# One 512-column product for a weight block's high half and both halves of the activations

## The chip, the core and the metric

The kernel runs on one core of a Trainium2 chip. The metric is the time of one execution on the device in microseconds (us). Inside the core five engines work side by side, each through its own queue in order: PE (TensorE, matrix products; PEld is its weight loads), DVE (VectorE), ACT (ScalarE), POOL (GpSimd) and SP (here the queue that issues the DMAs).

## The reference

Two layers over 256 tokens of width 2048. Each layer has a mixer sub-layer (two attentions, gates, projections) and a feed-forward with a depthwise convolution of width 3; both take an input that is RMS-normalised and modulated by the conditioning vector `c` (adaLN). The change lies in the feed-forward alone:

```python
h = rmsnorm(x, norm_ffn[l]) * (1.0 + sc_m) + sh_m
u = depthwise_conv(h @ w_up[l], conv_w[l], conv_b[l])   # 2048 -> 2 x 5632
g, v = jnp.split(u, 2, axis=-1)
x = x + gt_m * ((jax.nn.silu(g) * v) @ w_down[l])       # 5632 -> 2048
```

All inputs are float32.

## The kernel before

**Layout.** Activations lie with features on the 128 partitions and the 256 tokens (`S`) along the row, in chunks of 128 features. Weights come as blocks of 128 x 128; 16 blocks (1 MB) are a *unit*, loaded by one DMA into a tile `w` (line 335) of a pool of four, which the adaLN weights share. A layer's units follow each other in the order in which the products use them (`block_stream`); a layer has 232 units, and its feed-forward is units 100 to 231.

**Two halves.** To keep float32 accuracy from the faster fp32r products, each operand is split in a high half (rounded) and a low half (the rest). For weights `unit_steps` does this in two pieces of 8 blocks: ACT casts the high half (line 346), DVE subtracts to get the low half (line 347), both into a tile `hl`, of which there are four, so two units' worth. A block's contribution is high x high + high x low + low x high: three products of 256 columns in `feature_block` (lines 375 to 377), accumulated over the blocks of one output column in one of four PSUM tiles `ps`. The activation operand is read "turned": columns alternate between the first and the second 128 tokens (`turns`), and the sums come back by `turned_back` or are already in order (`sorted`).

**The feed-forward.** The 44 chunks of hidden features go in three groups of 14, 17 and 13. A group's up-projection takes for each chunk a g column and a v column of 128 features, 16 blocks each, so one unit a column. Evacuation of a column (`g_evac`, `v_evac`, `conv`): ACT computes u = w1 ps + b (line 1096), DVE adds the two neighbour taps by two multiply-adds (line 1098); for g, ACT applies silu (1126); for v, DVE multiplies by silu(g) (1131), and `split` makes the two halves of `act` (ACT 452, DVE 455). The group's down-projection then runs over the 16 output chunks, the first three together, and DVE adds each to the residual stream `x` (`residual`, line 1071). The first 12 of the 28 columns of the first group work on `bare`, the input before normalisation, with two extra columns for the shift (258, 256 and 258 columns); the rest use the normalised `h`. The feed-forward's last group in layer 0 also feeds the squares and the bare chunks for the next layer; in layer 1 each output chunk is stored by a DMA.

**The order.** A scheduler in the framework sorts the instructions when the program is built; each engine's queue then runs in that order. The adaLN weights `aw` of layer 1 stream in by a plan of counts by unit (`ADA_PLAN_0`: 80 by unit 108, 143 by unit 231), each followed by a DVE product of 128 x 2048 (line 246).

Of the kernel before, what the change touches and what calls it, by code (L numbers as in the profile page):

```python
# [9 lines left out]
F32 = mybir.dt.float32  # L10
F32R = mybir.dt.float32r
AF = mybir.ActivationFunctionType
ALU = mybir.AluOpType
AX = mybir.AxisListType

P = 128
L = 2
D = 2048
S = 256
# [65 lines left out]

SCORES_3 = (1,)
EARLY = {1: 2}

MOVED_QK = [(), (0,1,2,8)]
QK_STEPS = 3  # L90
# [53 lines left out]
def encoder(ctx: ExitStack, tc: tile.TileContext, a: dict, out: bass.AP):  # L144
    nc = tc.nc
# [13 lines left out]
    ev = pool("ev", 3)  # L159
# [30 lines left out]
    sp = pool("s", 1)  # L190
# [13 lines left out]
    def led(name, apart=None):  # L204

        t = hp.tile([P, KC * 2 * S + OFF + ROW], F32R, name=name, tag="h")
        at = [0] + [OFF + 2 * S * k for k in range(1, KC)]
        if apart:
            at[apart] += ROW - OFF
            at[apart + 1 :] = [i + ROW for i in at[apart + 1 :]]  # L210
        return [t[:, i : i + 2 * S].rearrange("p (a s) -> p a s", a=2) for i in at]
# [55 lines left out]
    class Paced:  # L267


        def __init__(self):  # L270
            self.jobs, self.later = [], []
# [87 lines left out]
    def turns(columns):  # L359

        return columns.rearrange("p (r q) -> p q r", r=2)

    def turned_back(columns):

        return columns.rearrange("p (q r) -> p r q", r=2)

    def pair(columns):

        return columns.rearrange("p (r q) -> p r q", r=2)

    def feature_block(ps, hl, j, act, first, last):

        hi, lo = hl[:, 0, j * P : (j + 1) * P], hl[:, 1, j * P : (j + 1) * P]
        out = ps[:, : 2 * act[0].shape[1]]
        nc.tensor.matmul(out, hi, act[0], start=first, stop=False)  # L375
        nc.tensor.matmul(ps[:, :S], hi, act[1], start=False, stop=False)  # L376
        nc.tensor.matmul(out, lo, act[0], start=False, stop=last)  # L377

    class Stream:
# [33 lines left out]
        def features(self, acts, evacs, late=None, at={}, sorted=False):  # L413

            pss = [mm.tile([P, 512], F32, name=f"ps{self.l}_{self.u}_{self.at}_{m}", tag="mm") for m in range(len(evacs))]
            for i, act in enumerate(acts):
                if late and i == len(acts) - LATE:
                    late()
                if i in at:
                    at[i]()  # L420
                for ps in pss:
                    hl, j = self.next_block()
                    act_of = act if isinstance(act, tuple) else (turns(act[:, 0]), turns(act[:, 1]))
                    feature_block(ps, hl, j, act_of, i == 0, i == len(acts) - 1)
                    if self.at == UB:
                        self.tick()
            for ps, evac in zip(pss, evacs):
                evac(ps[:, : S + 2] if isinstance(acts[0], tuple) else ps[:, :S] if sorted else turned_back(ps[:, :S]))

        def tokens(self, h, kcs):  # L430

# [16 lines left out]

    def split(dst, src, scale=None, held=False):

        if scale is None:
            high = nc.scalar.copy(dst[:, 0], src)
            if held:
                tc.keep_in_program_order(high)
            nc.vector.tensor_tensor(out=dst[:, 1], in0=src, in1=dst[:, 0].bitcast(F32), op=ALU.subtract)
            return
        nc.scalar.activation(out=dst[:, 0], in_=src, func=AF.Copy, scale=scale)
        nc.vector.scalar_tensor_tensor(
            out=dst[:, 1], in0=src, scalar=scale, in1=dst[:, 0].bitcast(F32), op0=ALU.mult, op1=ALU.subtract
        )  # L460
# [64 lines left out]
    def normed(l, w, h, rbs):  # L525

        mod, amod = mods[l], amods[l]
        for kc in range(KC):
            t = ev.tile([P, S], F32, name="ht", tag="z")
            sh = mod[:, 3 * w * KC + kc : 3 * w * KC + kc + 1]  # L530
            nc.vector.scalar_tensor_tensor(
                out=t[:], in0=x[:, kc], scalar=amod[:, w, kc : kc + 1], in1=rbs[:], op0=ALU.mult, op1=ALU.mult
            )
            hi, lo, src = h[kc][:, 0], h[kc][:, 1], t[:]
            if w:
                hi, lo, src = turns(hi), turns(lo), src.rearrange("p (q r) -> p q r", r=2)
            nc.scalar.activation(out=hi, in_=src, func=AF.Identity, bias=sh)  # L537
            nc.vector.scalar_tensor_tensor(  # L538
                out=lo, in0=src, scalar=sh, in1=hi.bitcast(F32), op0=ALU.add, op1=ALU.subtract
            )  # L540
            yield
# [6 lines left out]
    class Bare:  # L548
# [42 lines left out]
        def roots(self):  # L591
            self.rbs = spread(self.rs)
            self.h = led(f"h{self.l}_{self.w}")
            self.steps = normed(self.l, self.w, self.h, self.rbs)
            bg.add(self.steps, H_RATE[self.w])

# [259 lines left out]
    for l in range(L):  # L856
# [17 lines left out]
        if l:  # L874
# [13 lines left out]
            h = bare.h  # L888
# [85 lines left out]
        for pi, (groups, gates) in enumerate(parts):  # L974
            last = pi == len(parts) - 1
            for g, part in enumerate(groups):
# [16 lines left out]
                def turned(g=g):  # L993
                    ready[0] = g + 1
# [72 lines left out]
        def residual(ps, mo, part):  # L1067

            gt = mod[:, part * KC + mo : part * KC + mo + 1]
            to = pair(x[:, mo])  # L1070
            nc.vector.scalar_tensor_tensor(out=to, in0=ps, scalar=gt, in1=to, op0=ALU.mult, op1=ALU.add)

        sums = Squares(f"ssm{l}")
        bare = Bare(l, 1, sums)
# [27 lines left out]
        for gi, chunks in enumerate(FF_GROUPS):  # L1102
            acts = []
            homes = [(tag, n) for tag, n in (("a", 12), ("b0", 12), ("b1", 12))] if gi % 2 else [("o", 16), ("y0", 4), ("y1", 4), ("y2", 4)]

            def act_of(c):

                while len(acts) <= c - chunks[0]:
                    tag, n = homes.pop(0)
                    acts.extend(chunks_of(sp, tag, n // 2, f"act{l}_{gi}_{tag}", min(n // 2, len(chunks) - len(acts)), False))  # L1110
                return acts[c - chunks[0]]

            sil = {}

            def level(ps):

                if ps.shape[-1] == S:
                    return ps
                z, sh = bare.level(ps)
                nc.scalar.activation(out=z[:], in_=z[:], func=AF.Identity, bias=sh[:, :1])  # L1120
                return z[:]

            def g_evac(ps, c):
                u = sil[c] = paired(F32, "u")
                conv(level(ps), c, u[:, 0])
                nc.scalar.activation(out=u[:, 0], in_=u[:, 0], func=AF.Silu)

            def v_evac(ps, c):
                u = sil.pop(c)
                conv(level(ps), FC + c, u[:, 1])  # L1130
                nc.vector.tensor_tensor(out=u[:, 1], in0=u[:, 1], in1=u[:, 0], op=ALU.mult)
                split(act_of(c), u[:, 1])

            sets = [[c] for c in chunks]
            if gi == 0:
                sets = [chunks[: SIDE // 2]] + sets[SIDE // 2 :]
            for cs in sets:
                fns = [lambda p, e=e, c=c: e(p, c) for c in cs for e in (g_evac, v_evac)]
                src = bare.chunks if gi == 0 and cs[0] < BARE[1] // 2 else bare.h
                if len(cs) > 1:  # L1140
                    st.features(src, fns, at=bare.at())
                else:
                    for fn in fns:
                        st.features(src, [fn], sorted=True)
                if gi == 0 and cs[-1] == BARE[1] // 2 - 1:
                    bg.finish(bare.steps)
            if gi == len(FF_GROUPS) - 1:
                sums = Squares(f"ssf{l}") if l < L - 1 else None
                if sums:
                    over = Bare(l + 1, 0, sums)  # L1150
            else:
                sums = None
            last = gi == len(FF_GROUPS) - 1

            def down(mo):
                def evac(ps):
                    need(l, 80 + mo + 1)
                    residual(ps, mo, 5)
                    if last:
                        if l < L - 1:  # L1160
                            sums.add(mo)
                            over.add(mo)
                        else:
                            nc.sync.dma_start(out[:, mo], x[:, mo])

                return evac

            for mos in OUT_TURNS:
                end = mos[0] == KC - 1
                ending = last and mos[0] >= ENDING  # L1170
                if last and end and l < L - 1:
                    nxt = Stream(l + 1)
                    nxt.prefetch(AHEAD)
                with urgent(ending):
                    st.features(acts[: len(chunks)], [down(mo) for mo in mos], sums.first if sums and end else None)
# [77 lines left out]
```

## Time and profile before

| | before |
|---|---|
| three runs, median | 2604.09 us (2602.87 to 2605.14) |
| profiled execution, time | 2603.6 us |
| its span, first to last instruction | 2601.8 us |
| granted TensorE clock | 0.998 |
| read from HBM | 695 MB |
| layer 0's feed-forward (from its first bare product to the next layer's) | 610.8 to 1322.8 us |
| layer 1's feed-forward | 1885.5 to 2596.7 us |

Rows of the profile read: line, engine, operation, output tile <- input tiles, shape, count, then busy us and mean ns of one, then the engine's idle time ahead of it with who ended it. Rows of the timeline begin with start and duration in us. On DVE and ACT the start of the next instruction can lie up to 0.1 us before the end of the one ahead.

### The profile page before, as it was taken

To read this page: it belongs to the slowest core of one execution; us is meant where nothing else is said; L and a number is where in the kernel's file an instruction comes from. 1 tells how busy PE (TensorE), PEld (TensorE's weight loads), DVE (VectorE), ACT (ScalarE), POOL (GpSimd) and SP (SyncE) were. 2 spreads that over 40 slices of the span, in tenths; PEclk is the share of its full clock that TensorE was granted. 3 is DMA by queue.
4 is the path that set the end of the run, shared out by engine and by line. 5 is a ranking of instruction groups with operands and counts; after the bars stand their busy time and mean duration, and the time that the engine had idled before them with its cause. 6 is when DMAs were issued, how large, how long until landed. Compare 5 with 4: busy or idle time off the path is not lost.

```text
span 2601.8 us, 51007 instructions
## 1 busy us (share of the span) xinstructions
PE 2574.4 (99%) x21164; PEld 2507.9 (96%) x21164; DVE 2122.7 (82%) x2979; ACT 1404.2 (54%) x2280; POOL 247.9 (10%) x345
## 2 busy tenths in 40 slices
PE   8999999999999999999999999999999999999999
PEld 6999899999999999999998889999999999999999
DVE  8998998998987888788987778878888876655664
ACT  5445765456653555355565666645575445544553
POOL 0001100000000000000003668620000000000000
PEclk9999999999999999999999999999999999999999
DMA  9998779885787777777866656777757775555554
GB/s 370 353 353 302 262 295 358 331 315 213 275 309 289 301 297 299 303 292 292 298 239 256 252 220 253 255 272 274 288 177 293 289 268 200 200 197 195 195 197 144
DMA packets 102186, 700.47 MB, mean 269 GB/s; under 512 B 12865, under 2 KB 15169, under 8 KB 18113
## 3 DMA queue, kind: packets, MB, share of 16 engines
q1 hardware_dynamic: 101954, 697.20, 72.5%
q8 instruction: 166, 2.72, 0.4%
q14 instruction: 66, 0.54, 0.1%
HBM read 695.06 MB, written 2.10 MB: 268 GB/s over the span
## 4 chain that ended last, share of the span: by engine, by line
PE 78%; DVE 9%; DMA 4%; ACT 3%; POOL 3%; issue 3%; SPq 0%; DVEq 0%; POOLq 0%; ACTq 0%
PE ps L377 23%; PE ps L375 23%; PE ps L376 23%; DVE hl L347 3%; DMA aw<-in_aw 3%; PE ps_t L440 2%; PE ps_t L441 2%; PE ps_t L442 2%; DVE aw L246 2%; ACT hl L346 1%; POOL packA L318 1%; POOL p L318 1%; DMA w<-in_ws 1%; PE sc L691 1%; POOL qrs L506 1%
## 5 line engine op out<-in xcount | busy, mean ns | idle before, releaser
L347 DVE TENSOR_TENSOR hl<-w,hl 128x1024 fp32r<-128x1024 f32 x928 | 1132.2, 1226 | 293.4 <-ACT hl L346 290.9
L346 ACT CAST hl<-w 128x1024 fp32r<-128x1024 f32 x928 | 965.6, 1046 | 692.9 <-PE ps L377 504.9
L375 PE MATMUL ps<-h,hl 128*128 128x256 f32 x3328 | 916.1, 275 | 1.9 <-DVE ri L709 0.8
L376 PE MATMUL ps<-h,hl 128*128 128x256 f32 x3328 | 915.2, 275 | 0.0
L377 PE MATMUL ps<-h,hl 128*128 128x256 f32 x3328 | 914.6, 275 | 0.0
L375 PEld LDWEIGHTS ps<-h,hl 128*128 128x128 f32 x3328 | 638.8, 192 | 3.1 <-ACT hl L346 0.9
L376 PEld LDWEIGHTS ps<-h,hl 128*128 128x128 f32 x3328 | 638.9, 192 | 0.4 <-DVE h L538 0.2
L377 PEld LDWEIGHTS ps<-h,hl 128*128 128x128 f32 x3328 | 638.6, 192 | 0.0
L246 DVE CUSTOM_DVE_ANT_0 aw<-aw,cact,ab 128x2048 f32<-128x2048 f32 x189 | 444.0, 2350 | 12.1 <-DMA aw<-in_aw 11.7
L440 PE MATMUL ps_t<-hl,h 128*128 128x512 f32 x576 | 218.2, 384 | 4.4 <-ACT h L537 2.7
L441 PE MATMUL ps_t<-hl,h 128*128 128x512 f32 x576 | 220.1, 383 | 1.5 <-DVE hl L347 1.4
L442 PE MATMUL ps_t<-hl,h 128*128 128x512 f32 x576 | 219.1, 381 | 0.0
L1098 DVE SCALAR_TENSOR_TENSOR u<-ps,cw,u 128x255 f32<-128x255 f32 x304 | 146.4, 481 | 86.4 <-ACT u L1096 82.0
L1096 ACT ACTIVATE u<-ps,cw 128x256 f32<-128x256 f32 x152 | 85.8, 564 | 198.6 <-PE ps L377 198.6
L377 PE MATMUL ps<-merged,hl 128*128 128x256 f32 x512 | 141.0, 276 | 0.9 <-DVE hl L347 0.9
L375 PE MATMUL ps<-merged,hl 128*128 128x256 f32 x512 | 140.6, 275 | 0.8 <-DVE m L468 0.8
L376 PE MATMUL ps<-act_o,hl 128*128 128x256 f32 x512 | 140.8, 275 | 0.0
L377 PE MATMUL ps<-act_o,hl 128*128 128x256 f32 x512 | 140.8, 275 | 0.0
L376 PE MATMUL ps<-merged,hl 128*128 128x256 f32 x512 | 140.7, 275 | 0.0
L375 PE MATMUL ps<-act_o,hl 128*128 128x256 f32 x512 | 140.5, 275 | 0.0
L440 PEld LDWEIGHTS ps_t<-hl,h 128*128 128x128 f32 x576 | 109.4, 191 | 21.3 <-ACT h L537 3.7
L441 PEld LDWEIGHTS ps_t<-hl,h 128*128 128x128 f32 x576 | 109.7, 191 | 18.7 <-DVE hl L347 3.7
(244 smaller groups left out, 4847.5 us busy)
## 6 DMA issues: line engine op xcount, KB each, us to landing
w<-in_ws SPq DMA_DIRECT2D x463, 1024.0 KB, 4.9
aw<-in_aw SPq DMA_DIRECT2D x189, 1024.0 KB, 5.3
p<-in_bias SPq DMA_DIRECT2D x16, 256.0 KB, 4.6
x<-in_xT SPq DMA_DIRECT2D x4, 512.0 KB, 5.3
aw_o<-in_aw SPq DMA_DIRECT2D x2, 1024.0 KB, 12.3
out<-x SPq DMA_DIRECT2D x16, 128.0 KB, 3.1
w<-in_ws SPq DMA_DIRECT2D x2, 512.0 KB, 11.6
aw_b<-in_aw SPq DMA_DIRECT2D x1, 1024.0 KB, 18.3
```

The costliest lines, as they stand in the source:

```text
L246: product = nc.vector.tensor_tensor_reduce(out=raw[:], in0=raw[:], in1=cact[:], scale=1.0, scalar=ab[:, i : i + 1], op0=ALU.mult, op1=ALU. ...
L318: nc.gpsimd.tensor_copy(out=dst[a : a + BLOCK, :, :, b : b + BLOCK], in_=src[b : b + BLOCK, :, :, a : a + BLOCK])
L346: nc.scalar.copy(hl[:, 0], r)
L347: nc.vector.tensor_tensor(out=hl[:, 1], in0=r, in1=hl[:, 0].bitcast(F32), op=ALU.subtract)
L375: nc.tensor.matmul(out, hi, act[0], start=first, stop=False)
L376: nc.tensor.matmul(ps[:, :S], hi, act[1], start=False, stop=False)
L377: nc.tensor.matmul(out, lo, act[0], start=False, stop=last)
L440: nc.tensor.matmul(ps[:], xh, hi, start=kc == kcs[0], stop=False)
L441: nc.tensor.matmul(ps[:], xh, lo, start=False, stop=False)
L442: nc.tensor.matmul(ps[:], xl, hi, start=False, stop=kc == kcs[-1])
L1096: nc.scalar.activation(out=u, in_=ps, func=AF.Identity, scale=w[:, 1:2], bias=w[:, 3:4])
L1098: nc.vector.scalar_tensor_tensor(out=u[:, to], in0=ps[:, of], scalar=w[:, j : j + 1], in1=u[:, to], op0=ALU.mult, op1=ALU.add)
```

## The change

For h (behind the bare columns) and for the act chunks of both layers, a chunk's two halves are laid out so that one operand of 512 columns, `both`, holds the 256 turned columns of the high half and then those of the low half (`Wide`). A block is two products: its high half with `both` (512 columns, one whole PSUM tile), its low half with `high` (256 columns, added to the first 256 sums). The two sums are added at evacuation: for an up column ACT copies the second to SBUF (`both`, in the tag of `z`) and DVE adds the first, and `conv` works from SBUF; a down column takes two residual multiply-adds.

```diff
+BOTH_HALVES = (0,1)
...
+    class Wide:
+        def __init__(self, chunk):
+            columns = chunk.rearrange("p a s -> p (a s)")
+            quarters = columns.rearrange("p (r a q) -> p a r q", r=2, a=2)
+            self.halves = [quarters[:, a] for a in range(2)]
+            self.both = turns(columns)
+            self.high = self.halves[0].rearrange("p r q -> p q r")
...
     def feature_block(ps, hl, j, act, first, last):
         hi, lo = hl[:, 0, j * P : (j + 1) * P], hl[:, 1, j * P : (j + 1) * P]
+        if isinstance(act, Wide):
+            nc.tensor.matmul(ps[:], hi, act.both, start=first, stop=False)
+            nc.tensor.matmul(ps[:, :S], lo, act.high, start=False, stop=last)
+            return
...
-                evac(ps[:, : S + 2] if isinstance(acts[0], tuple) else ps[:, :S] if sorted else turned_back(ps[:, :S]))
+                wide = isinstance(acts[0], Wide)
+                sums = [ps[:, a * S : (a + 1) * S] for a in range(1 + wide)]
+                if not sorted:
+                    sums = [turned_back(p) for p in sums]
+                evac(ps[:, : S + 2] if isinstance(acts[0], tuple) else sums if wide else sums[0])
...
+        if isinstance(dst, Wide):
+            hi, lo = dst.halves
+            nc.scalar.copy(hi, pair(src))
+            nc.vector.tensor_tensor(out=lo, in0=pair(src), in1=hi.bitcast(F32), op=ALU.subtract)
+            return
...
-            nc.vector.scalar_tensor_tensor(out=to, in0=ps, scalar=gt, in1=to, op0=ALU.mult, op1=ALU.add)
+            for p in ps if isinstance(ps, list) else [ps]:
+                nc.vector.scalar_tensor_tensor(out=to, in0=p, scalar=gt, in1=to, op0=ALU.mult, op1=ALU.add)
...
             def level(ps):
+                if isinstance(ps, list):
+                    z = ev.tile([P, S], F32, name="both", tag="z")
+                    nc.scalar.copy(z[:], ps[1])
+                    nc.vector.tensor_tensor(out=z[:], in0=ps[0], in1=z[:], op=ALU.add)
+                    return z[:]
```

The scheduler sorts the changed instructions anew. In the second up-projection of layer 0 (units 142 to 179) DVE's queue had this for one pair of columns, g in `ps0_150` and v in `ps0_151` (hl0_152_1 is the low half of unit 152's second piece; the ISA rows are the product with the adaLN weights):

```order
L347 TENSOR_TENSOR hl0_152_0_10111<-w0_152_10109,hl0_152_0_10111 128x1024
L1098 SCALAR_TENSOR_TENSOR u_10038<-ps0_150_16_0_9979,cw0_997,u_10038 128x255
L347 TENSOR_TENSOR hl0_152_1_10114<-w0_152_10109,hl0_152_1_10114 128x1024
L1098 SCALAR_TENSOR_TENSOR u_10038<-ps0_150_16_0_9979,cw0_997,u_10038 128x255
L347 TENSOR_TENSOR hl0_153_0_10175<-w0_153_10173,hl0_153_0_10175 128x1024
L1098 SCALAR_TENSOR_TENSOR u_10038<-ps0_151_16_0_10043,cw0_997,u_10038 128x255 x2
L347 TENSOR_TENSOR hl0_153_1_10178<-w0_153_10173,hl0_153_1_10178 128x1024
L1131 TENSOR_TENSOR u_10038<-u_10038 128x256
L246 ISA aw1_6_10165,mod1_9454<-aw1_6_10165,cact_100,ab1_9455 128x2048
L246 ISA mod1_9454 128x1
L455 TENSOR_TENSOR act0_1_a_9589<-u_10038,act0_1_a_9589 128x256
```

The same pair on DVE after the change, where line 349 is the low half, 1158 the add of the two sums, 1135 the multiply-add, 1174 the product with silu(g), 478 the low half of act and 248 the adaLN product:

```order
L349 TENSOR_TENSOR hl0_152_0_9565<-w0_152_9563,hl0_152_0_9565 128x1024
L1174 TENSOR_TENSOR u_9400<-u_9400 128x256
L1158 TENSOR_TENSOR both_9503<-ps0_150_16_0_9459,both_9503 128x256
L349 TENSOR_TENSOR hl0_152_1_9568<-w0_152_9563,hl0_152_1_9568 128x1024
L478 TENSOR_TENSOR act0_1_a_9147<-u_9400,act0_1_a_9147 128x2x128
L1135 SCALAR_TENSOR_TENSOR u_9502<-both_9503,cw0_997,u_9502 128x255
L349 TENSOR_TENSOR hl0_153_0_9616<-w0_153_9614,hl0_153_0_9616 128x1024
L1135 SCALAR_TENSOR_TENSOR u_9502<-both_9503,cw0_997,u_9502 128x255
L1158 TENSOR_TENSOR both_9553<-ps0_151_16_0_9510,both_9553 128x256
L349 TENSOR_TENSOR hl0_153_1_9619<-w0_153_9614,hl0_153_1_9619 128x1024
L1135 SCALAR_TENSOR_TENSOR u_9502<-both_9553,cw0_997,u_9502 128x255
L248 ISA aw1_6_9603,mod1_9037<-aw1_6_9603,cact_100,ab1_9038 128x2048
```

The second multiply-add of g moved from ahead of one low half (hl0_153_0) to behind it, one instruction ahead of the next low half (hl0_153_1).

ACT's queue at the same place before:

```order
L1096 ACTIVATE u_10038<-ps0_150_16_0_9979,cw0_997 128x256
L346 CAST hl0_152_1_10114<-w0_152_10109 128x1024
L346 CAST hl0_153_0_10175<-w0_153_10173 128x1024
L1126 ACTIVATE u_10038<-u_10038 128x256
L1096 ACTIVATE u_10038<-ps0_151_16_0_10043,cw0_997 128x256
L346 CAST hl0_153_1_10178<-w0_153_10173 128x1024
```

And after, with the copy in line 1157, the cast of the weights in 348, the high half of act in 477, u in 1133 and silu in 1169:

```order
L1157 COPY both_9503<-ps0_150_16_0_9459 128x256
L348 CAST hl0_152_1_9568<-w0_152_9563 128x1024
L477 CAST act0_1_a_9147<-u_9400 128x2x128
L1133 ACTIVATE u_9502<-both_9503,cw0_997 128x256
L348 CAST hl0_153_0_9616<-w0_153_9614 128x1024
L1157 COPY both_9553<-ps0_151_16_0_9510 128x256
L1169 ACTIVATE u_9502<-u_9502 128x256
L348 CAST hl0_153_1_9619<-w0_153_9614 128x1024
```

Silu (1169) stands directly ahead of the cast of hl0_153_1; before, the u of the v column stood between them.

More of the change, by code (lines that the diff above doesn't have):

```diff
@@ L369, in pair, with turned @@
         return columns.rearrange("p (r q) -> p r q", r=2)
+    class Wide:
[5 more added lines that the diff above has]
+            self.high = self.halves[0].rearrange("p r q -> p q r")
+        def turned(self):
+            return [half.rearrange("p r q -> p q r") for half in self.halves]
     def feature_block(ps, hl, j, act, first, last):
         hi, lo = hl[:, 0, j * P : (j + 1) * P], hl[:, 1, j * P : (j + 1) * P]
+        if isinstance(act, Wide):
+            nc.tensor.matmul(ps[:], hi, act.both, start=first, stop=False)
+            nc.tensor.matmul(ps[:, :S], lo, act.high, start=False, stop=last)
+            return
         out = ps[:, : 2 * act[0].shape[1]]
@@ L422, in features @@
                     hl, j = self.next_block()
-                    act_of = act if isinstance(act, tuple) else (turns(act[:, 0]), turns(act[:, 1]))
+                    act_of = act if isinstance(act, (tuple, Wide)) else (turns(act[:, 0]), turns(act[:, 1]))
                     feature_block(ps, hl, j, act_of, i == 0, i == len(acts) - 1)
@@ L533, in normed @@
             )
-            hi, lo, src = h[kc][:, 0], h[kc][:, 1], t[:]
-            if w:
-                hi, lo, src = turns(hi), turns(lo), src.rearrange("p (q r) -> p q r", r=2)
+            src = t[:]
+            if isinstance(h[kc], Wide):
+                hi, lo = h[kc].turned()
+                src = src.rearrange("p (q r) -> p q r", r=2)
+            else:
+                hi, lo = h[kc][:, 0], h[kc][:, 1]
+                if w:
+                    hi, lo, src = turns(hi), turns(lo), src.rearrange("p (q r) -> p q r", r=2)
             nc.scalar.activation(out=hi, in_=src, func=AF.Identity, bias=sh)
@@ L593, in roots @@
             self.h = led(f"h{self.l}_{self.w}")
+            if self.w and self.l in BOTH_HALVES:
+                self.h = [Wide(c) for c in self.h]
             self.steps = normed(self.l, self.w, self.h, self.rbs)
@@ L1109, in act_of @@
                     tag, n = homes.pop(0)
-                    acts.extend(chunks_of(sp, tag, n // 2, f"act{l}_{gi}_{tag}", min(n // 2, len(chunks) - len(acts)), False))
+                    new = chunks_of(sp, tag, n // 2, f"act{l}_{gi}_{tag}", min(n // 2, len(chunks) - len(acts)), False)
+                    acts.extend([Wide(c) for c in new] if l in BOTH_HALVES else new)
                 return acts[c - chunks[0]]
```

## The prediction

> **What bounds the kernel now.** I read the page from the top: busy shares, then the chain that ended last, then the feed-forward stages one by one, then single rows of TensorE and of the two evacuating queues.
>
> ```profile
> span 2601.8 us, 51007 instructions
> PE 2574.4 (99%) x21164; PEld 2507.9 (96%) x21164; DVE 2122.7 (82%) x2979; ACT 1404.2 (54%) x2280; POOL 247.9 (10%) x345
> ...
> PE 78%; DVE 9%; DMA 4%; ACT 3%; POOL 3%; issue 3%; SPq 0%; DVEq 0%; POOLq 0%; ACTq 0%
> ```
>
> TensorE is busy for 99% of the span and carries 78% of the chain, so a shorter product shortens the kernel, unless the queue behind it runs out first. That queue is DVE at 82%, an average. By stage (columns: stretch, its length, then busy time and count of PE, PEld, DVE, ACT, POOL, granted clock, DMA share, GB/s):
>
> ```profile
> 840.00:1022.00 182.00, 182.00 (x1632) 182.00 (x1632) 159.06 (x211) 96.75 (x134) 0.00 (x0) 1.00 0.80 301
> 1022.00:1113.00 91.00, 91.00 (x817) 91.00 (x817) 69.33 (x81) 37.60 (x46) 0.00 (x0) 1.00 0.80 303
> 1253.00:1322.00 69.00, 69.00 (x621) 69.00 (x620) 62.73 (x86) 37.95 (x58) 0.00 (x0) 1.00 0.82 302
> 2114.00:2296.00 182.00, 182.00 (x1632) 182.00 (x1632) 124.55 (x168) 98.09 (x134) 0.00 (x0) 1.00 0.58 203
> ```
>
> These are layer 0's second up-projection, second down-projection and last down-projection, and layer 1's second up-projection. TensorE has no gap in any, at full clock. DVE's share is 87%, 76%, 91% and 68%: layer 0 is tight, since the adaLN products (aw) of layer 1 run under it; layer 1 is loose.
>
> What sets TensorE's pace inside a block? Three rows and a pair:
>
> ```profile
> L377 PE MATMUL ps<-h,hl x544: 275/275/275, 840.6 to 1022.5; 128*128 128x256 f32 x182
> ...
> 1930.35 0.28 PE L377 MATMUL ps<-bare_b,hl 128*128 128x258 f32 x1
> 1953.13 0.28 PE L377 MATMUL ps<-bare_y,hl 128*128 128x258 f32 x1
> ...
> 1930.34:1953.12 22.78, 18.77 (x68) 12.99 (x69) 1.00 0.70 237
> ...
> L442 PE MATMUL ps_t<-hl,h x144: 379/379/379, 1368.1 to 1460.7; 128*128 128x512 f32 x144
> ```
>
> First row: 543 steps from block to block in 181.9 us, 335.0 ns each, so 111.7 ns for a product of 256 columns. The pair with its window: 68 blocks of 258, 256 and 258 columns in 22.78 us, again 335.0 ns. Four columns more cost nothing, so the columns do not set this pace; each product has one weight load, and the load does. Last row: 143 steps of three 512-column products in 92.6 us, 215.8 ns each, 107.9 ns per 256 columns. That operand also steps 256 numbers from column to column, as the new `both` does. So a 512-column product hides its neighbour's load and a 256-column product is stretched by it.
>
> [...]
>
> **The change, part by part.** *Products.* A block goes from three products with three loads to two with two. In the 44 chunks of a layer 88 up columns less 12 from the bare input are wide, times 16 blocks, plus 44 x 16 down blocks: 1216 + 704 = 1920, 3840 in two layers. The wide product costs 215.8 (L442). The 256-column one is followed by the load of the next block's weights, so I take 111.7; its lower bound is half the 512 row, 107.9. The block: 327.5 ns, between 323.7 and 327.5. Saved: 7.5 x 3840 = **28.8 us** (bounds 28.8 and 43.4), if the loads' pace is the whole reason.
>
> *Evacuation, up.* 152 columns each gain an ACT copy and a DVE add, and the activation and both multiply-adds then read SBUF; the multiply-add takes 479 ns from SBUF (from lev, just below) and 0.48 us from PSUM (from ps, further below), so I count no change there.
>
> ```profile
> L1023 ACT COPY ya<-ps 128x256 f32<-128x256 f32 x16 | 5.8, 370 | 11.5 <-PE ps L377 11.5
> L605 DVE TENSOR_TENSOR lev<-ps,rbs 128x256 f32<-128x256 f32 x11 | 4.4, 419 | 0.0
> L1098 DVE SCALAR_TENSOR_TENSOR u<-lev,cw,u 128x255 f32<-128x255 f32 x21 | 9.9, 479 | 1.0 <-ACT u L1096 0.8
> ```
>
> On ACT 0.37 us a column lies beside other work (layer 0's stage has it busy 97 of 182 us). On DVE it does not. One pair of columns (g and v) in layer 0 now, DVE first, then ACT:
>
> ```profile
> 950.45 0.42 DVE L1131 TENSOR_TENSOR u<-u 128x256 f32<-128x256 f32 x1
> 950.78 2.35 DVE L246 CUSTOM_DVE_ANT_0 aw<-aw,cact,ab 128x2048 f32<-128x2048 f32 x1
> 953.05 0.42 DVE L455 TENSOR_TENSOR act_b<-u,act_b 128x256 fp32r<-128x256 f32 x1
> 953.46 1.22 DVE L347 TENSOR_TENSOR hl<-w,hl 128x1024 fp32r<-128x1024 f32 x1
> 954.60 0.48 DVE L1098 SCALAR_TENSOR_TENSOR u<-ps,cw,u 128x255 f32<-128x255 f32 x1
> 954.99 1.22 DVE L347 TENSOR_TENSOR hl<-w,hl 128x1024 fp32r<-128x1024 f32 x1
> 956.12 0.48 DVE L1098 SCALAR_TENSOR_TENSOR u<-ps,cw,u 128x255 f32<-128x255 f32 x1
> 956.94 1.23 DVE L347 TENSOR_TENSOR hl<-w,hl 128x1024 fp32r<-128x1024 f32 x1 [0.34 <-ACT hl L346]
> 959.09 1.00 DVE L1098 SCALAR_TENSOR_TENSOR u<-ps,cw,u 128x255 f32<-128x255 f32 x2 [0.92 <-ACT u L1096]
> 960.02 1.23 DVE L347 TENSOR_TENSOR hl<-w,hl 128x1024 fp32r<-128x1024 f32 x1
> 961.16 0.42 DVE L1131 TENSOR_TENSOR u<-u 128x256 f32<-128x256 f32 x1
> ...
> 950.45 1.05 ACT L346 CAST hl<-w 128x1024 fp32r<-128x1024 f32 x1 [1.18 <-PE ps L377]
> 956.80 0.41 ACT L1126 ACTIVATE u<-u 128x256 f32<-128x256 f32 x1
> 1312.84 0.42 ACT L486 ACTIVATE sq<-x 128x256 f32<-128x256 f32 x1 [2.16 <-DVE x L1071]
> 1313.16 0.50 ACT L578 ACTIVATE bare_b<-x,amod 128x256 fp32r<-128x256 f32 x1
> ```
>
> From L1131 to L1131 are 10.71 us, two of TensorE's units of 5.36. Starts show what an instruction really occupies: 1.13 for hl, 0.39 for a multiply-add, 0.33 for a 256-column add. The two waits are 0.42 and 1.02 us by starts (956.51 to 956.94, 958.07 to 959.09); without them DVE works 9.27 us. After: two adds bring 0.66, and the multiply-adds no longer stand back to back, which saves 0.12 (1.00 against 2 x 0.48, less overlap): 9.81 us of work. TensorE's new pace is 32 x 0.3275 = 10.48. That would fit, but the order changes where DVE waits. In most of layer 0 the new queue has the second multiply-add of g, the add of v, and then the weight half whose cast stands on ACT behind the silu, which needs that multiply-add. From its start: 0.48, then 0.32 of ACT for the silu (1312.84 to 1313.16 is one such step), 1.05 for the cast, two handovers of about 0.03 (ACT's u ends as the wait at 959.09 does): 1.91; DVE fills 0.39 + 0.33 of it. So 1.19 us of wait that lateness does not absorb: 11.0 us a pair, 0.52 over TensorE's pace. DVE becomes the bound there.
>
> A half has slack first: cast at 950.45 when its buffer comes free, low half ready at 954.68, and TensorE wants it three halves later (3 x 2.62 = 7.86 by the new pace); less the two adds, about 3 us. In the first such stage (units 150 to 177, 14 pairs) 7.3 - 3 = 4.3 us come through; in the third group's 12 pairs, three of which also have the copy in the loop (its 0.37 less the overlap, 0.3 more), 7.1 - 3 = 4.1. The first group and the first pairs of the second have another DVE hl inside the loop: no wait. Bounds of both together: 0, if the slack were larger or the silu earlier; 45 under the second rival.
>
> Layer 1 has the same loop without most aw: 124.55/17 + 0.66 + 1.2 = 9.2 us a pair, under 10.48. Nothing.
>
> *Evacuation, down.* 96 residuals become two multiply-adds, 0.39 to 0.52 more each. Second group of layer 0: 69.3 + 16 x 0.4 = 75.7 of 89: hidden. Last down of layer 0: 62.7 + 6.2 to 8.3 = 69 to 71 against 208 x 0.3275 = 68.1; the idle two units before it refill the slack, so I take 1.0 (0 to 3).
>
> *Ends.* The last residual stands ahead of the last output, and another ahead of layer 1's first norm. A second multiply-add on the same x is 1.00 - 0.48 = 0.52: 1.0 for both.
>
> *Writes into the wide layout.* The high and low writes of h and act keep their counts and go in runs of 128; `bare` is written in two runs of 128 already, at 0.48 (the L578 row, ACT 0.50). Nothing. The DMA list is the same but for one small load that moves a place.
>
> Sum: -28.8 + 4.3 + 4.1 + 1.0 + 1.0 = -18.4 us. The profiled execution took 2603.6 us (the median shown is 2604.09, 0.5 above): **2585.2 us**.
>
> **The rivals.**
> (1) DVE keeps up in layer 0. For it: work alone is 9.81 of 10.48. Against: the loop through silu. 2603.6 - 28.8 + 1.0 = 2575.8.
> (2) Slower, by one mechanism: DVE keeps today's 1.44 us of waits and gets the 1.19 on top, 12.4 us a pair. For it: the waits are on ACT, which gets more to do in the same queue. Against: today's waits follow TensorE, and a late DVE would not meet them. Over 26 pairs (12.4 - 10.48) x 26 - 6 = 44 us, so 2603.6 - 28.8 + 44 + 2 = 2621. It turns the result slower by over 0.2% from 11.9 us a pair.
> (3) The change doesn't do what it says: the wide product from h or act takes two loads' time, 223 ns, a block stays at 335. Then DVE falls short by only 0.28 a pair: some 4 us in all, 2608. Against it stands the L442 row, whose operand has the same step. [...]
> (4) The 256-column product goes at its columns' pace: 323.8 a block, 43 us saved; DVE's deficit grows to 0.64 a pair, 15 us lost in all: 2575.
>
> **How the numbers follow.** Forecast 0.62 (own range 2580 to 2592), rival 1 0.14, rival 4 0.08, rival 2 0.05, rival 3 0.08, and 0.03 for DVE losses of 15 to 24 us. The range runs from just below rivals 1 and 4 to just short of rival 3: 2573 to 2598. A measurement of this kernel tells 0.2%, about 5 us, from no change. Faster: 0.62 + 0.14 + 0.08 + 0.03 = 0.87. Same: rival 3, 0.08. Slower: rival 2, 0.05.
>
> **What the new profile would show.** Wide and narrow products in turn, a block at 327.5 ns in layer 1's feed-forward with no PE idle; there about 14.4 us are gone. In layer 0's second and third up-projection PE waits on DVE hl once a pair, from the seventh pair or so, and DVE waits about 1.2 us on ACT hl ahead of the half behind the silu. Wrong would be the pace, if layer 1 does not give 14 us; the loop, if layer 0's up stages show no PE wait or one from the first pair on.

## The result and the profile after

The changed kernel takes 2588.7 us (median of six runs, 2583.21 to 2589.95) against 2604.61 us before (six runs, 2602.09 to 2608.84). The ratio is 0.9934 with a 95% interval of 0.9922 to 0.9947: faster by 0.66%, 15.9 us. The forecast was 2585.2, between 2573 and 2598. The profiled execution of after took 2583.2 us, 5.5 under the median of its runs; some of that is ahead of the first feed-forward, which it reached after 608.1 us, where profiled executions of kernels with the same code up to there took 608.1 to 616.3. So stages are compared here by their own length.

The page of after begins so:

```profile
span 2581.4 us, 43559 instructions
PE 2549.9 (99%) x17324; PEld 2377.2 (92%) x17324; DVE 2209.4 (86%) x3227; ACT 1450.7 (56%) x2432; POOL 246.0 (10%) x345
...
PE 67%; DVE 19%; ACT 5%; issue 4%; POOL 3%; DMA 3%; ACTq 0%; DVEq 0%; POOLq 0%; SPq 0%
```

3840 products and as many weight loads are gone. TensorE is busy for 99% of the span, as before, but its share of the chain fell from 78 to 67%, while DVE's rose from 9 to 19%. Where DVE took over is seen by stage, the same four as in the prediction:

```profile
834.00:1015.00 181.00, 179.43 (x1087) 163.38 (x1086) 163.12 (x239) 103.57 (x163) 0.00 (x0) 1.00 0.78 292
1015.00:1105.00 90.00, 89.71 (x545) 81.74 (x544) 79.69 (x105) 39.70 (x51) 0.00 (x0) 1.00 0.85 322
1244.00:1318.00 74.00, 70.40 (x417) 62.52 (x417) 72.13 (x109) 40.32 (x61) 0.00 (x0) 1.00 0.82 297
2106.00:2284.00 178.00, 178.00 (x1089) 163.61 (x1089) 139.19 (x204) 108.59 (x167) 0.00 (x0) 1.00 0.58 207
```

The last row, layer 1's second up-projection, has TensorE busy for all of it. The three above, layer 0's, have gaps, and in the last down-projection of layer 0 DVE is busy for 72.1 of 74 us. TensorE's waits in layer 0's wide stages (who waited for whom: total in us, times, longest):

```profile
PE ps L392 <- DVE hl L349: 5.6, 15, 1.2
PE ps L391 <- ACT hl L348: 0.6, 1, 0.6
PE ps L391 <- DVE act_y L478: 0.4, 1, 0.4
```

These rows count TensorE's idle time alone, 6.6 us. By the starts of the products (0.57 us lost at the wait that ended at 950.17 us, where the rows have 0.30 us of idle time) the wide stages of layer 0 took 12.4 us more than TensorE's pace.

The length of each stage, from its first product to the next stage's first, in us, with those of the experiments below (TensorE's pace is the number of blocks times 327.5 ns):

| layer 0 | before | after | pace | e2 order | e3 fewer aw | e4 narrow | e5 both |
|---|---|---|---|---|---|---|---|
| up 1 (normalised part) | 85.76 | 83.84 | 83.84 | 83.84 | 83.84 | 83.84 | 83.84 |
| down 1 | 75.04 | 73.36 | 73.36 | 73.36 | 73.37 | 73.36 | 73.57 |
| up 2 | 182.24 | 181.46 | 178.16 | 178.16 | 179.31 | 181.52 | 178.16 |
| down 2 | 91.12 | 90.12 | 89.08 | 89.08 | 89.08 | 90.13 | 89.08 |
| up 3 | 139.36 | 138.29 | 136.24 | 136.24 | 136.24 | 138.53 | 136.24 |
| down 3 | 69.68 | 74.08 | 68.12 | 69.81 | 68.12 | 72.15 | 68.12 |
| feed-forward, with the bare part | 712.00 | 709.96 | 697.6 | 699.28 | 698.01 | 708.33 | 697.80 |

Layer 1's feed-forward with all that follows to the end of the program went from 716.29 to 700.87 us, with every wide stage at TensorE's pace; layer 0's went from 712.00 to 709.96.

### The profile page after: what moved, and what is told of

It is laid out like the page before. It is cut to its first block, busy times and chain, and to the rows that moved or that the text cites. A ratio compares the mean times of both kernels' runs of the same rounds, so it can differ in the third digit from the quotient of the medians.

```text
span 2581.4 us, 43559 instructions
## 1 busy us (share of the span) xinstructions
PE 2549.9 (99%) x17324; PEld 2377.2 (92%) x17324; DVE 2209.4 (86%) x3227; ACT 1450.7 (56%) x2432; POOL 246.0 (10%) x345
## 4 chain that ended last, share of the span: by engine, by line
PE 67%; DVE 19%; ACT 5%; issue 4%; POOL 3%; DMA 3%; ACTq 0%; DVEq 0%; POOLq 0%; SPq 0%
PE ps L391 24%; PE ps L392 12%; DVE hl L349 8%; PE ps L397 7%; PE ps L395 7%; PE ps L396 7%; DVE aw L248 3%; ACT hl L348 3%; PE ps_t L466 2%; PE ps_t L465 2%; PE ps_t L464 2%; DVE u L1135 1%; DMA w<-in_ws 1%; POOL packA L320 1%; POOL p L320 1%
## 5 line engine op out<-in xcount | busy, mean ns | idle before, releaser
L391 PE MATMUL ps<-h,hl 128*128 128x512 f32 x2432 | 797.4, 382 | 0.0
L392 PE MATMUL ps<-h,hl 128*128 128x256 f32 x2432 | 664.0, 273 | 2.8 <-DVE hl L349 2.8
L391 PEld LDWEIGHTS ps<-h,hl 128*128 128x128 f32 x2432 | 459.7, 189 | 63.7
L392 PEld LDWEIGHTS ps<-h,hl 128*128 128x128 f32 x2432 | 466.9, 192 | 5.7 <-DVE hl L349 5.6
L395 PE MATMUL ps<-h,hl 128*128 128x256 f32 x896 | 247.3, 276 | 1.9 <-DVE ri L745 0.8
L396 PE MATMUL ps<-h,hl 128*128 128x256 f32 x896 | 246.4, 275 | 0.0
L397 PE MATMUL ps<-h,hl 128*128 128x256 f32 x896 | 245.8, 275 | 0.0
L395 PEld LDWEIGHTS ps<-h,hl 128*128 128x128 f32 x896 | 171.9, 192 | 3.1 <-ACT hl L348 1.0
L396 PEld LDWEIGHTS ps<-h,hl 128*128 128x128 f32 x896 | 172.0, 192 | 0.4 <-DVE h L572 0.2
L391 PE MATMUL ps<-act_o,hl 128*128 128x512 f32 x512 | 171.1, 382 | 0.6 <-ACT hl L348 0.6
L397 PEld LDWEIGHTS ps<-h,hl 128*128 128x128 f32 x896 | 171.6, 192 | 0.0
L1135 DVE SCALAR_TENSOR_TENSOR u<-both,cw,u 128x255 f32<-128x255 f32 x304 | 146.0, 480 | 2.9
L392 PE MATMUL ps<-act_o,hl 128*128 128x256 f32 x512 | 139.9, 273 | 1.6 <-DVE hl L349 1.6
```

The lines of the kernel that those rows point to most:

```text
L391: nc.tensor.matmul(ps[:], hi, act.both, start=first, stop=False)
L392: nc.tensor.matmul(ps[:, :S], lo, act.high, start=False, stop=last)
L1135: nc.vector.scalar_tensor_tensor(out=u[:, to], in0=ps[:, of], scalar=w[:, j : j + 1], in1=u[:, to], op0=ALU.mult, op1=ALU.add)
```

## The experiments

The theory: a product's weight load sets TensorE's pace, two products under two loads take 7.5 ns less than three under three (327.5 against 335.0), and in layer 0 DVE gives most of it back, by waiting in a loop through silu and by more work in the last down-projection.

**e1: the change in layer 1 alone.**

```diff
-BOTH_HALVES = (0,1)
+BOTH_HALVES = (1,)
```

> Only layer 1's feed-forward uses the wide operand; layer 0 is as before. Theory (the weight load of each product sets TensorE's pace, and DVE eats the gain in layer 0 alone): layer 1's feed-forward falls from 711.1 to 696.8 us (1920 blocks x 7.5 ns = 14.4), layer 0's stays at 712.0, no TensorE wait for a low half in layer 0's wide stages; 2604.6 - 14.4 = 2590.2 us, within 2 us of the full change, since layer 0 gave only 2.0 us there. Rival (the gain is spread evenly over both layers and the lost part is a cost common to both): about half the full change's gain, 2596.5 us.

2592.3 us (ratio to before 0.9953, 0.9940 to 0.9967). Layer 0's feed-forward took 712.0 us, as before, and layer 1's 696.8 from its first product with a bare chunk to its last product (711.1 before): the 14.4 us that the theory expected. The 2590.2 expected lies inside its runs (2589.7 to 2594.7); the evenly spread gain (2596.5) does not. Layer 0's half of the change brought 2.0 us in its own stages. By median e1 lies 3.6 us above the full change, where at most 2 were expected; the highest run of the full change (2589.95) and the lowest of e1 (2589.69) meet, so the runs do not tell more about this half than the stages do.

**e2: silu held behind the v column's u.** `keep_in_program_order` makes the scheduler leave an instruction where the program has it.

```diff
 def conv(ps, ch, u):
...
-    nc.scalar.activation(out=u, in_=ps, func=AF.Identity, ...)
+    lead = nc.scalar.activation(out=u, in_=ps, func=AF.Identity, ...)
+    if l == 0 and gi and ch >= FC:
+        tc.keep_in_program_order(lead)
...
 def g_evac(ps, c):
...
-    nc.scalar.activation(out=u[:, 0], in_=u[:, 0], func=AF.Silu)
...
 def v_evac(ps, c):
...
     conv(level(ps), FC + c, u[:, 1])
+    gate = nc.scalar.activation(out=u[:, 0], in_=u[:, 0], func=AF.Silu)
+    if l == 0 and gi:
+        tc.keep_in_program_order(gate)
```

> The full change with ACT's silu of the second and third groups of layer 0 held behind the v column's u, so that the next weight cast no longer stands behind it; every instruction and its work stays. Theory (the 1.19 us wait of DVE in the loop multiply-add, silu, cast, low half makes the pair 11.0 us): pairs go back under TensorE's 10.48 us, TensorE's waits for low halves in the second and third up-projection of layer 0 (3.3 and 2.1 us lost) and the one behind the second (1.0) vanish, and the last down-projection starts with slack; layer 0's feed-forward falls by 6 to 8 us, about 2582 us in all. Rival (DVE is simply full, its work sets the pair, whatever the order): no change, 2588.7 us, waits as before.

2577.4 us (ratio to before 0.9899, 0.9883 to 0.9914), 11.3 us under the full change, where 6 to 8 were expected. DVE's waits for weight casts in the second up-projection, first of after, then of e2:

```profile
DVE hl L349 <- ACT hl L348: 17.0, 17, 1.2
```

```profile
DVE hl L349 <- ACT hl L348: 8.5, 17, 0.9
```

And the stage by e2's windows, DVE busy for 168.3 of 178 us, with TensorE at its pace:

```profile
834.00:1012.00 178.00, 178.00 (x1089) 163.85 (x1088) 168.31 (x243) 106.70 (x164) 0.00 (x0) 1.00 0.82 302
```

Both later up-projections and the second down-projection are at TensorE's pace, and the last down-projection fell by 4.3 us: the stages of layer 0 give 10.7 us. So DVE was not full: the same work in another order fits. The expectation had counted the three waits (6.4 us) and left out most of the 4.3.

**e3: 15 adaLN products less under layer 0's feed-forward.**

```diff
-ADA_PLAN_0 = [..., (108, 80), (231, 143)]
-ADA_PLAN_1 = [(8, 143), (76, 166), ...]
+ADA_PLAN_0 = [..., (108, 80), (231, 128)]
+ADA_PLAN_1 = [(8, 128), (76, 166), ...]
```

> The full change with 15 of the 63 adaLN products of layer 1 that run under layer 0's feed-forward moved into layer 1's attention (the plan's corner 143 becomes 128 at the end of layer 0). Theory (DVE is the bound of layer 0's feed-forward): a pair has 0.78 of such a product in place of 1.02, 2.27 us each, so 10.5 us against TensorE's 10.48; TensorE's waits in the up-projections nearly vanish (5.4 us less), the last down-projection gains 2 to 3 us; layer 0's feed-forward falls by 7 to 9 us, layer 1's attention rises by 0 to 5; 2581 to 2587 us. Rival (layer 0's losses are TensorE's own, for example the wide operand against transfers into SBUF): layer 0 stays within 2 us of the full change, 2588 us or above.

Layer 0's feed-forward fell to 698.0 us, 12 under the full change (7 to 9 expected), with the last down-projection at its pace. The 1.15 us left over the pace in the second up-projection fall at 839.5 us, the stage's start, and not in the loop. But the whole took 2592.2 us (ratio to before 0.9954, 0.9940 to 0.9968), outside the expected 2581 to 2587: from layer 0's end to layer 1's feed-forward it took 578.3 us where after had 562.5. There TensorE's waits for low halves in layer 1's attention rose, first after, then e3:

```profile
PE ps_t L465 <- DVE hl L349: 0.3, 1, 0.3
```

```profile
PE ps_t L465 <- DVE hl L349: 7.4, 4, 3.4
```

The expected 0 to 5 us for the new place of the products came to 15.8. These waits are 7.1 us of it, and a later one for a low half (at 1686.1 us) 2.2. A part of the rest is the clock: between the two feed-forwards the records show four stretches of 3.4 us at a granted clock of 0.50 in e3, from 1461.4, 1512.6, 1522.9 and 1686.7 us on, and one in after. Three of the four begin within 1.3 us of the end of such a wait. In 3 us TensorE ran 16 products in one of them (first row, e3) and 29 at the full clock in the same window of after (second row):

```profile
1687.00:1690.00 3.00, 3.00 (x16) 3.00 (x16) 2.48 (x8) 1.47 (x5) 2.79 (x6) 0.50 0.98 396
```

```profile
1687.00:1690.00 3.00, 3.00 (x29) 3.00 (x29) 3.00 (x5) 1.05 (x1) 2.83 (x5) 1.00 0.90 317
```

The theory on layer 0 held: with less work a pair fits too, as it does with another order (e2). The price of the place to which the work went was missed.

**e4: the last down-projection of layer 0 as before.**

```diff
-acts.extend([Wide(c) for c in new] if l in BOTH_HALVES else new)
+acts.extend([Wide(c) for c in new] if l in BOTH_HALVES and (l, gi) != (0, 2) else new)
```

> The full change with the last down-projection of layer 0 left as before: three products a block, one residual multiply-add, act in the old layout. Theory (that stage is bound by DVE, which 16 more residuals overload): it goes from 74.1 us back to 69.7 plus the wait at its entry of about 1.5 us, so 3 to 4.5 us less in that stage, 2584 to 2586 us. Rival (its 6 us over TensorE's pace come from the lateness that the up-projection hands over): the stage stays at 73 us or more, 2588 us or above.

2587.6 us (ratio to before 0.9937, 0.9921 to 0.9952): by time not told apart from the full change. The stage fell by 1.9 us to 72.15, between the theory's 71.2 and the rival's 73. Without any extra residual it was still 2.5 us longer than before, waiting for one low half at its start and for the last act chunk:

```profile
PE ps L397 <- DVE hl L349: 1.0, 1, 1.0
PE ps L396 <- DVE act_y L484: 0.3, 1, 0.3
```

That is lateness that the up-projection handed over. So both causes are in the 6 us; e2 and e5 size them.

**e5: e2, with the adaLN plan bent inside layer 0's feed-forward.**

```diff
-ADA_PLAN_0 = [..., (108, 80), (231, 143)]
+ADA_PLAN_0 = [..., (108, 80), (222, 141), (231, 143)]
```

> The second run's order (silu behind the v column's u) with the adaLN plan bent inside layer 0's feed-forward: 141 of the 143 products by unit 222, so that the last down-projection has about four fewer. Theory (what is left over TensorE's pace there, 69.8 against 68.1 us, is DVE's work): that stage falls to 68.1 to 68.5 us, the others keep TensorE's pace, since a pair works 9.9 of 10.48 us; about 2576 us. Rival (the rest is the handover from the up-projection or the end of the layer): it stays at 69.8, 2577.4 us.

The stage fell from 69.81 in e2 to 68.12 us, exactly TensorE's pace, so the rest there, 1.7 us, was DVE's work. All of layer 0's wide stages together are now within 0.3 us of the pace. The row of the stage:

```profile
1238.00:1306.00 68.00, 68.00 (x417) 62.54 (x416) 64.55 (x99) 38.21 (x58) 0.00 (x0) 1.00 0.75 273
```

The time is 2576.2 us (ratio to before 0.9888, 0.9870 to 0.9906), the best median here; 1.2 us under e2 is less than the runs can tell.

**e6 and e7: columns cut, loads kept.** e6 is before with a narrower second product, e7 is after with a narrower last product, in both projections of layer 1's second and third groups (there `cut[0]` is true). Each ran once: 2601.5 and 2592.9 us. What they tell is in their stages.

```diff
 # e6
-nc.tensor.matmul(ps[:, :S], hi, act[1], start=False, stop=False)
+few = act[1][:, :64] if cut[0] else act[1]
+nc.tensor.matmul(ps[:, : P if cut[0] else S], hi, few, start=False, stop=False)
 # e7
-nc.tensor.matmul(ps[:, :S], lo, act.high, start=False, stop=last)
+few = act.high[:, :64] if cut[0] else act.high
+nc.tensor.matmul(ps[:, : P if cut[0] else S], lo, few, start=False, stop=last)
```

> The kernel before, with the second product of a block (high half with the low activations) over 128 of its 256 columns in the second and third groups of layer 1; the low activations of the other columns are left out there. Theory (each product's weight load sets the pace): a block stays at 335.0 ns, the second up-projection of layer 1 at 182.2 us. [...]

> The full change, with the narrow product (low half of the weights) over 128 of its 256 columns in the second and third groups of layer 1; the low weights of the other tokens are left out there. Theory (the narrow product is stretched by the load behind it): a block stays at 327.5 ns, the second up-projection of layer 1 at 178.2 us. Rival (the narrow product goes at its columns' pace once a wide one stands beside it): the block falls by 53 ns, that stage to 149 us.

The second up-projection of layer 1 in e6 (count, then shortest, median and longest duration in ns, first and last start), the cut product and the last one of a block, and then the cut product in e7:

```profile
L379 PE MATMUL ps<-h,hl x543: 221/222/223, 2114.1 to 2295.6; 128*128 128x128 f32 x181
...
L380 PE MATMUL ps<-h,hl x544: 328/328/329, 2113.8 to 2295.7; 128*128 128x256 f32 x182
```

```profile
L395 PE MATMUL ps<-h,hl x544: 219/219/220, 2115.8 to 2293.6; 128*128 128x128 f32 x182
```

In e6, 181.9 us from the first block's last product to the last one's: 335.0 ns a block. In e7 177.8 us: 327.4 ns, which is the 327.5 of after within the tenth of a us of these rows. The stages took 182.24 and 178.11 us, as with 256 columns (182.24 and 178.16). Halving a product's columns saves no time in either. At the pace of the 512-column row in the prediction (107.9 ns for 256 columns) the 128 columns would have been an estimated 54 ns a block, and the two stages 152.9 and 148.8 us; the rival of e7 had 53 and 149. Both stages are far from that.

One rival is in no expectation: a least time of 111.7 ns for each product, whatever is loaded. Every product here has one load, so the counts can't tell. The starts in e6 can (L379 is the cut product, PEld are the loads):

```profile
2149.90 0.22 PE L379 MATMUL ps<-h,hl 128*128 128x128 f32 x1
2149.90 0.19 PEld L380 LDWEIGHTS ps<-h,hl 128*128 128x128 f32 x1
2149.96 0.33 PE L380 MATMUL ps<-h,hl 128*128 128x256 f32 x1
2150.01 0.19 PEld L377 LDWEIGHTS ps<-h,hl 128*128 128x128 f32 x1
2150.12 0.28 PE L377 MATMUL ps<-h,hl 128*128 128x256 f32 x1
2150.12 0.19 PEld L379 LDWEIGHTS ps<-h,hl 128*128 128x128 f32 x1
2150.23 0.22 PE L379 MATMUL ps<-h,hl 128*128 128x128 f32 x1
2150.24 0.19 PEld L380 LDWEIGHTS ps<-h,hl 128*128 128x128 f32 x1
```

The product behind the cut one starts 0.06 us after it, so there is no such least time. The next then starts 0.16 us later and the one after it 0.11. The loads start 0.11, 0.11 and 0.12 us apart all the same (110 to 113 ns throughout the stage), and the products wait for them.

## Why the prediction was right, point by point

**The pace: right.** The 28.8 us came from 7.5 ns a block, by way of the load. After has, in layer 1's second up-projection, 543 blocks in 177.9 us:

```profile
L392 PE MATMUL ps<-h,hl x544: 272/273/273, 2106.0 to 2283.9; 128*128 128x256 f32 x182
```

That is 327.6 ns by rows of a tenth of a us, 327.5 by the stage's length. Layer 1's wide stages gave 14.4 us, the forecast figure. The choice of the load's 111.7 ns for the narrow product, not its columns' 107.9, is shown by the block and by e7, though only as part of the sum. By the recorded starts the wide product begins 0.11 us after the narrow one in after and the next narrow one 0.22 after that; in e7 it is 0.05 and 0.27:

```profile
2149.87 0.22 PE L395 MATMUL ps<-h,hl 128*128 128x128 f32 x1
2149.92 0.43 PE L393 MATMUL ps<-h,hl 128*128 128x512 f32 x1
2150.19 0.22 PE L395 MATMUL ps<-h,hl 128*128 128x128 f32 x1
```

Rivals 3 (no gain) and 4 (columns' pace) fall with the block's 327.5. So does a pace by columns in the kernel before: e6 took 128 columns from a block, an estimated 54 ns at the pace of the 512-column row, and the block kept its 335.0.

**The loop in layer 0: right in place and size.** DVE in after, in the pair that the prediction walked through:

```profile
948.88 1.23 DVE L349 TENSOR_TENSOR hl<-w,hl 128x1024 fp32r<-128x1024 f32 x1
950.02 0.43 DVE L1174 TENSOR_TENSOR u<-u 128x256 f32<-128x256 f32 x1
...
953.69 0.48 DVE L1135 SCALAR_TENSOR_TENSOR u<-both,cw,u 128x255 f32<-128x255 f32 x1
954.08 0.42 DVE L1158 TENSOR_TENSOR both<-ps,both 128x256 f32<-128x256 f32 x1
955.66 1.23 DVE L349 TENSOR_TENSOR hl<-w,hl 128x1024 fp32r<-128x1024 f32 x1 [1.16 <-ACT hl L348]
...
959.87 1.22 DVE L349 TENSOR_TENSOR hl<-w,hl 128x1024 fp32r<-128x1024 f32 x1
961.00 0.42 DVE L1174 TENSOR_TENSOR u<-u 128x256 f32<-128x256 f32 x1
```

and ACT beside it:

```profile
954.27 0.42 ACT L1169 ACTIVATE u<-u 128x256 f32<-128x256 f32 x1 [1.64 <-DVE u L1135]
954.59 1.04 ACT L348 CAST hl<-w 128x1024 fp32r<-128x1024 f32 x1
```

The multiply-add ends at 954.17, silu starts at 954.27, the cast ends at 955.63 and DVE's low half starts at 955.66. From L1174 to L1174 are 10.98 us; 11.0 was forecast, with a wait of 1.19 (1.16 in the row). TensorE stands once a pair, not for this low half but for the next one, which DVE makes behind the adaLN product (at 948.88 and at 959.87 us, done at 950.11 and 961.09):

```profile
950.17 0.38 PE L392 MATMUL ps<-h,hl 128*128 128x256 f32 x1 [0.30 <-DVE hl L349]
961.14 0.38 PE L392 MATMUL ps<-h,hl 128*128 128x256 f32 x1 [0.23 <-DVE hl L349]
```

By the products' starts TensorE loses 0.57 us at the first and 0.49 at the second; the forecast was 0.52 a pair. The first such wait in that stage was at 939.1 us, behind the sixth of DVE's long waits (the seventh pair or so was forecast). Rival 1 (DVE keeps up) fell by these rows. Rival 2 (the waits of before on top, 12.4 us a pair) fell too: 11.0.

**The sum: the losses were put in the wrong stages.** By the stages of the profiled executions:

| term | forecast | measured |
|---|---|---|
| products | -28.8 | -14.4 in layer 1 (after); -14.2 in layer 0 when DVE is out of the way (e5) |
| up 2 of layer 0 | +4.3 | +3.3 |
| down 2 of layer 0 | 0 | +1.0 |
| up 3 of layer 0 | +4.1 | +2.05 |
| down 3 of layer 0 | +1.0 | +6.0 |
| ends | +1.0 | between -1.0 and +0.5 |

The step that failed is "the idle two units before it refill the slack, so I take 1.0 (0 to 3)". They did not, and the stage lost 6.0, outside that bound. TensorE meets the handed-over lateness 1.6 us into the down-projection, ahead of any refilling, with the longest of its waits there (1.2 us), and waits go on to 1312 us. Three runs take the two causes apart. With the lateness and without the additional residuals 2.5 us are lost over that stage's own pace (e4). With the residuals and without the lateness it is 1.7 (e2), and with fewer adaLN products beside them nothing (e5). Alone the two make 4.2 of the 6.0; the other 1.8 come only where a DVE that is late gets the additional work.

The lateness also cost the 1.0 us at the start of the second down-projection, put at nothing, which is gone in e2. In the third up-projection less came through than forecast: only three waits, the first at 1211 us. From one product with silu(g) to the next, DVE's first eight pairs there took 87.92 us, 4.1 over TensorE's pace, so the slack was about 4 us and not 3:

```profile
1123.03 0.42 DVE L1174 TENSOR_TENSOR u<-u 128x256 f32<-128x256 f32 x1
...
1210.95 0.42 DVE L1174 TENSOR_TENSOR u<-u 128x256 f32<-128x256 f32 x1
```

That the sum came so near is partly luck. The forecast put 3.1 us too much into the two up-projections and 6.0 too little into the two down-projections, and these errors offset each other in part. The pace and the loop were not luck: both came out in their places and sizes.

The ends were costed at 0.52 each. The last residual's second multiply-add is there (the pair takes 1.00 us), but the stretch from the start of layer 1's last down-projection to the end of the program fell from 74.73 to 72.12 us, by 2.6 us where the pace alone gives 1.6. e6, with its loads and all that follows the products as in before, took 73.16 us there, 1.6 less than before, so half a us there is inside the spread from run to run: against e6 the end cost 0.5 us, against before it gained 1.0. At the join of the layers nothing was lost (the stretch behind it, up to the first 256-column product with layer 1's h, took 249.7 against 249.9 us).

In all the products of the two feed-forwards took 16.4 us less in the profiled executions, where -28.8 + 12.4 gives the same; the forecast's was 18.4 with the ends.

## What to carry to other kernels

Here the weight loads set the pace of products of 256 columns (335.0 ns for three, and the same with 128 columns less), so loads were to be counted, not columns: joining two products under one load saved 7.5 ns a block with the columns the same. Before adding work to an engine that follows the bound at nearly 90%, walk once around its new queue with the neighbours: DVE's work alone would have fitted, one cast queued behind one silu made it late, and moving that silu was worth 11 us of median time, near the whole change's 16. Lateness left at the end of a stage was paid as the next one started (1.0 us at the second down-projection; 2.5 us in the last one of e4, which had no work added). Work moved out of a tight stage needs a stage that has room: here layer 1's attention did not have it (15.8 us longer up to layer 1's feed-forward in e3).

## What the runs showed of the hardware

Three products in a row, each behind a load of 128 x 128, took 335.0 ns whether all had 256 columns, two of them 258 (both in before), or one of them 128 (e6). In e6 the loads kept their 110 to 113 ns while the products started 0.06, 0.16 and 0.11 us apart, so the loads set the pace. A 512-column product and a narrow one took 327.5 ns together, with 256 columns in the narrow one (after) or 128 (e7). That is the 215.8 ns of a 512-column product with its load (before, line 442) and 111.7, a third of the 335.0. I read this as the wide one hiding the load for its neighbour, and the narrow one not.

Between the two feed-forwards e3's records show the granted clock at 0.50 four times for 3.4 us, three of them within 1.3 us of the end of a wait of TensorE for a low half, and those of after once (between 1518 and 1524 us). In one of e3's 16 products started in 3 us, where after had 29 at the full clock.

In the second up-projection of layer 0 DVE was 94.6% busy over 178 us in e2, and TensorE lost no time there. At 90% in after (163.1 of 181 us) it held TensorE up. A busy share does not tell which.

The eight products of 512 columns on float32 operands at the start of the kernel before (line 795) took 0.89 us each, from start to start (2.4 to 8.6 us); those on fp32r operands in line 442 took 215.8 ns.
